# Streams ordered by a per-form time estimate, gather steps paced in that time

## The chip, the cores and the metric

The kernel runs on one core of a Trainium2 chip. The metric is device microseconds of one execution. Its engines are PE (TensorE, matmuls), DVE (VectorE), ACT (ScalarE), POOL (GpSimd, which issues the gathers) and SP (which issues most loads). Each engine works through its own list of instructions in order; semaphores hold an instruction until what it reads is there.

## The reference, cut to what matters

One layer over 1024 tokens of width 1024, in float32:

```
x += W_out [ gated delta rule, 4 heads of 128, chunks | RG-LRU, 512 channels ](norm(x))
x += cross attention, 4 heads, into 256 memory tokens (norm(x))
x += PEER(norm(x)):
    sc = q . subkeys            # 8 heads x 2 halves x 128 keys
    top 16 of each half, top 16 of their sums -> 16 experts a head, 128 a token
    out = sum_e gate_e * gelu(u[e] . h) * v[e]      # u, v: 16384 x 1024
out = norm(x)
```

## The kernel before

The kernel is written as Python generators, called streams, which emit instructions piece by piece. A function `together` picks which stream emits next, while the program is built. A tile scheduler behind it may still move single instructions; what it makes of them is each engine's list.

**The front.** The stream `mixed` runs four mixers of 256 tokens (mixer 0 to 3). A mixer projects (`pj`), convolves, and then solves two chunks of 128 tokens one after the other. A chunk is a chain: a triangular inverse in levels of `gd` matmuls (operands `TT`, `Xi`, `Y`, `W`), whose results go through ACT copies (`Xi`, `Y`) and one DVE product (`W`, a 128x512 row) before the next matmuls can start. At its end stand `g`, `St`, `go` on DVE and a transposition (`tp<-identf,go`), and then the output projection, whose results DVE adds to `X`. Side streams do the RG-LRU channels. The stream `attended` does the cross attention and then the product-key queries (`pj<-hT,w` on PE, `sc`, top-16 searches `s`, `i`, `mr` on DVE) for units of tokens at 0, 128, 256, 512 and 768, each as soon as the mixer is through with it. After a unit a stream `choose` runs `select` on DVE (`cand`, `best`, `pos`, `mr`, `oh`, `e`), 128 tokens at a time: the final top 16 and the expert indices.

**Two ways to the experts.** Tokens 256 to 767 go the dense way. The stream `gated` builds with one-hot rows (`oh<-iot,e1T`, `oh<-keys,e2T` on DVE, `ohg` on ACT, `gd<-ohg,oh` on PE) a table of gates, which goes through `stage` to DRAM; this part is called the gates. Then `dense` runs 128 pieces, each with 24 `dh` and on average 24 `po` matmuls of 512 columns, in which every expert is computed for all 512 tokens. The other four blocks of 128 tokens (0, 128, 768, 896) go by gather steps, 256 a block, 1024 in all: POOL gathers 128 rows of u or v (512 KB) into one of six row buffers `rb`, and DVE does one row on it (SCALAR_TENSOR_TENSOR `rb`, 128x1024).

**What sets the order.** While it emits, the program keeps a clock of its own for each engine: `pe.at`, `act.at`, `dve.at`. `spend` adds an instruction's time, a fixed part and a rate by elements, from when its inputs are known; a result counts as known `HOP` later. `together` gives the turn to a stream whose time has come, by rank and by how much PE time it has had. `Paced.tick` adds up PE's time and emits a gather step (`step`) whenever another `pace` of it has passed: in the front of the time on the clock, waits too (`real`), in the dense phase of the matmuls' own time. `PACES` has one pace for each mixer, `PACE_G` that of the gates, `PACE_D` that of the dense phase. Steps left at the end run by themselves.

Of the kernel before, what the change touches and what calls it, by code (L numbers as in the profile page):

```python
# [8 lines left out]
F = mybir.dt.float32  # L9
BF = mybir.dt.bfloat16  # L10
# [3 lines left out]
AF = mybir.ActivationFunctionType  # L14
# [4 lines left out]
S = 1024  # L19
# [4 lines left out]
TD = 2 * T  # L24
# [9 lines left out]
BIG = 3.0e38  # L34
NROW = 6
RANK = (1, 1, 1, 0)
HOP, SLACK, WAIT = 100.0, 8000.0, 1000.0
SHARE = (6.0, 1.0, 6.0, 1.0)
L_NORM, L_STEP, L_CONV, L_SOFT, L_GATE = 14000.0, 2500.0, 4000.0, 6000.0, 1500.0
PACES = (2800.0, 2800.0, 2800.0, 3500.0)  # L40
PACE_G, PACE_D = 3500.0, 2250.0
FIRST = 0
EARLY = T
UNITS = ((0, 1), (128, 1), (256, 2), (512, 2), (768, 2))
CB = 2
# [4 lines left out]
def block_kernel(ctx: ExitStack, tc: tile.TileContext, a):  # L50
    nc = tc.nc
# [8 lines left out]
    def known(x):  # L60
        lo, hi = part(x)
        return max([t for (l, h), t in written.get(x.tensor.name, {}).items() if l <= hi and h >= lo],
                   default=0.0)

    def wrote(x, t):
        written.setdefault(x.tensor.name, {})[part(x)] = t

    def moved(n):
        dma[0] = max(dma[0], pe.at) + n / 360.0
        return dma[0] + 2000.0  # L70

    class Engine:

        def __init__(self, engine, fixed, rate):
            self.engine, self.fixed, self.rate = engine, fixed, rate
            self.at = self.total = self.end = 0.0

        def __getattr__(self, op):
            call = getattr(self.engine, op)

            def f(*args, **kw):
                r = call(*args, **kw)  # L82
                aps = [x for x in list(args) + list(kw.values()) if isinstance(x, bass.AP)]
                if op == "dma_start":
                    moved(prod(args[0].shape) * 4)
                else:
                    self.spend(aps)
                return r
            return f

        def spend(self, aps, n=0):
            t0 = max([self.at] + [known(x) for x in aps[1:]])
            ns = self.fixed + self.rate * (n or max(prod(x.shape[1:]) for x in aps))
            self.at = t0 + ns
            self.end = max(self.end, self.at)
            self.total += ns
            wrote(aps[0], self.at + HOP)

    class Paced(Engine):

        def __init__(self):
            super().__init__(nc.tensor, 0.0, 0.0)
            self.ns, self.pace, self.real = 0.0, PACES[0], True

        def matmul(self, out, l, r, **kw):
            self.engine.matmul(out, l, r, **kw)  # L106
            self.rate = 1.67 if r.dtype == F else 0.42
            self.tick([out, l, r])

        def transpose(self, out, i, ident):  # L110
            self.engine.transpose(out, i, ident)  # L111
            self.rate = 0.43
            self.tick([out, i])

        def tick(self, aps):
            t = self.at, self.total
            self.spend(aps, prod(aps[-1].shape[1:]))
            self.ns += self.at - t[0] if self.real else self.total - t[1]
            while self.ns > self.pace and (not self.real or dve.at < self.at + SLACK and not late_row()):
                self.ns -= self.pace  # L120
                step()

    pe = Paced()
    sp = Engine(nc.sync, 0.0, 0.0)
    act, dve = Engine(nc.scalar, 200.0, 0.72), Engine(nc.vector, 68.0, 1.04)

    consts = ctx.enter_context(tc.tile_pool(name="consts", bufs=1))
    small = ctx.enter_context(tc.tile_pool(name="small", bufs=2))
# [54 lines left out]
    def to_all(src, n):  # L183
        return bass.AP(tensor=src.tensor, offset=src.offset, ap=[[0, 128], [1, n]])
# [98 lines left out]
    def low(i):  # L283

        return early[:, 2 * i:2 * i + 2, :].rearrange("p s (c t) -> p (s c) t", c=D // T)
# [28 lines left out]
    def mm3(out, l, r, start, stop):  # L314
        pe.matmul(out, l[0], r[0], start=start, stop=False)
        pe.matmul(out, l[0], r[1], start=False, stop=False)
        pe.matmul(out, l[1], r[0], start=False, stop=stop)
# [96 lines left out]
    def mixer(fp, t0, qkv):  # L414
# [13 lines left out]
        hT = fp.tile([128, 8, T], F, name="hT", bufs=1)  # L428
        if t0 < EARLY:
            hT = Pair(hT, low(0), tmp)  # L430
# [4 lines left out]
        for c in range(8):  # L435
            if t0 < EARLY:
                mm3(ps[:8, :T], (wabh[:, c, :], wabl[:, c, :]), (hT.hi[:, c, :], hT.lo[:, c, :]), c == 0, c == 7)
# [85 lines left out]
        def out(b0, b1):  # L523

            while not ready >= {"y", *range(b0, b1)} or t0 and t0 not in read:
                yield None
            if not x1:
                x1.append(att.tile([128, NB, D], F, name="X1", bufs=1))
                sp.dma_start(x1[0], rows(a["x"], t0, NB))
            X = x1[0][:, b0:b1, :]  # L530
            for j in range(8):
                ps = yield from proj("wout", j, y, b1 - b0, b0)
                add_cols(X, j, ps)
            done[t0 + b0 * 128] = X
# [55 lines left out]
        for b in range(NB):  # L590
# [141 lines left out]
            if t0 == 0 and b == 0:  # L732
                yield Stream(out(0, 1), FIRST, SHARE[0])

# [368 lines left out]

    todo, fetched = [], []
    blocks = {}

    def add_block(row, rs, idx, gt):
# [5 lines left out]
    def row_of(i):  # L1115
        if not place:
            rb = gat.tile([128, NROW + 2, D], F, name="rb")
            place.extend(rb[:, k, :] for k in range(NROW + 2))
        return place[i]

    def slot():
        turn[0] += 1
        return row_of(turn[0] % NROW)

    def fetch():
        row, ph, k = todo.pop(0)
        B = blocks[row]
        if (ph, k) == ("u", 0):
            B["h"] = row_of(NROW)
            sp.dma_start(B["h"], x2d[row:row + 128, :])  # L1130
            B["w"] = slot()
            sp.dma_start(B["w"], to_all(a["wffn"], D))
        t = slot()
        pool.indirect_dma_start(  # L1134
            out=t, out_offset=None, in_=a[ph],
            in_offset=bass.IndirectOffsetOnAxis(ap=B["idx"][:, k:k + 1], axis=0))
        fetched.append((row, ph, k, t, moved(4.0 * 128 * D)))
# [4 lines left out]
    def step():  # L1142
        while todo and len(fetched) < NROW - 1:
            fetch()
        if not fetched:
            return False
        row, ph, k, t, _ = fetched.pop(0)
        B = blocks[row]
        if ph == "u":
            if k == 0:  # L1150
                dve.scalar_tensor_tensor(B["h"], B["h"], B["rs"], B["w"], op0=OP.mult, op1=OP.mult)
                B["hd"] = gat.tile([128, 128], F, name="hdot", bufs=1)
            tc.keep_in_program_order(
                dve.scalar_tensor_tensor(t, t, 1.0, B["h"], op0=OP.mult, op1=OP.mult,
                                         accum_out=B["hd"][:, k:k + 1]))
            if k == 120:
                B["x"] = row_of(NROW + 1)
                sp.dma_start(B["x"], x2d[row:row + 128, :])
            if k == 127:
                B["a"] = gat.tile([128, 128], F, name="ga", bufs=1)  # L1160
                act.activation(B["a"], B["hd"], AF.Gelu_apprx_tanh)
                dve.tensor_mul(B["a"], B["a"], B["gt"].rearrange("p h k -> p (h k)"))
        else:
            tc.keep_in_program_order(
                dve.scalar_tensor_tensor(B["x"], t, B["a"][:, k:k + 1], B["x"], op0=OP.mult, op1=OP.add))
            if k == 127:
                finish(B["x"], row, t)
        return True

    def finish(X, row, jk):  # L1170
        ss = small.tile([128, 1], F, name="f_ss")
        act.activation(jk, X, AF.Square, accum_out=ss)
        dve.tensor_scalar(ss, ss, 1.0 / D, EPS, op0=OP.mult, op1=OP.add)
        r = rsqrt(ss, 1, "f_")
        dve.scalar_tensor_tensor(X, X, r, wfin, op0=OP.mult, op1=OP.mult)
        sp.dma_start(a["out"][row:row + 128, :], X)
# [51 lines left out]
    def mixed():  # L1228

        for i in range(NP):  # L1230
            pe.pace = PACES[i]
            yield from mixer(fp, i * T, qkv)
# [10 lines left out]
    def attended():  # L1243
        yield from memory(att, KT, VM)
        first.rank = FIRST
        for t0, nb in UNITS:
# [17 lines left out]
    fps.close()  # L1264
    with tc.tile_pool(name="dn", bufs=1, side="right") as d2, \
            tc.tile_pool(name="dps", bufs=1, space=bass.MemoryType.PSUM) as dps:
        pe.pace, pe.real = PACE_D, False
        dense(dn[0], d2, dps, hT, raws)
    while step():
        pass  # L1270
# [64 lines left out]
```

## Time and profile before

| | |
|---|---|
| Median of 3 runs | 3278.47 us (3274.97 to 3279.72) |
| The profiled execution | 3275.43 us, its span 3273.7 us |
| PE, DVE, ACT, POOL busy | 91%, 84%, 39%, 44% of the span |
| First `dh` matmul | 1790 us |
| Last `po` matmul ends | 3261 us |

The profile is of one execution, and shares of it are means over stages that differ. The front is everything before the first `dh` matmul. A busy PE is not PE at its peak, since matmuls overlap in the records. Two rows of one engine may overlap by some 0.1 us, so a time from start to start says more than a duration.

### The profile page before, as it was taken

How to read it: one execution, taken by the hardware profiler on the slowest of the kernel's cores; microseconds unless marked ns; L12 is line 12 of the kernel's file. 1: busy time of each engine (PE TensorE's matmuls, PEld its weight loads, DVE VectorE, ACT ScalarE, POOL GpSimd, SP SyncE). 2: the span in 40 equal slices, each digit the busy share in tenths (PEclk: the TensorE clock that was granted, in tenths of full speed). 3: DMA queues.
4: the chain of work that ended last, by engine and by line, in shares of the span. 5: the costliest groups of instructions: out<-in, count | busy, mean ns of one | idle time of the engine just before them, and what ended most of it. 6: DMA issues, size and time to landing. Idle time of an engine off the chain costs nothing.

```text
span 3273.7 us, 46519 instructions
## 1 busy us (share of the span) xinstructions
PE 2987.4 (91%) x16212; PEld 2559.6 (78%) x16212; DVE 2737.6 (84%) x5999; ACT 1277.8 (39%) x2694; POOL 1431.4 (44%) x1046
## 2 busy tenths in 40 slices
PE   6999997699999989898857899999999999999998
PEld 6888887678988878887746677888888878888886
DVE  7634776877787898898999798888999989899998
ACT  6843363236322642376357332222222222222222
POOL 0000233334433344243345375556666655566663
PEclk9999998899999999998968899999999999999999
DMA  5346788688888769888888799999999899999995
GB/s 170 110 143 208 248 281 308 232 285 284 308 292 291 251 223 332 301 281 302 303 289 273 267 329 334 333 340 330 344 333 328 319 334 333 330 341 327 339 331 198
DMA packets 321547, 941.66 MB, mean 288 GB/s; under 512 B 28912, under 2 KB 108832, under 8 KB 319264
## 3 DMA queue, kind: packets, MB, share of 16 engines
q0 software_dynamic: 148048, 538.04, 46.8%
q1 hardware_dynamic: 107216, 367.08, 30.9%
q10 hardware_dynamic: 66048, 33.56, 3.7%
q8 instruction: 128, 2.10, 0.3%
q14 instruction: 107, 0.88, 0.1%
HBM read 894.53 MB, written 44.04 MB: 287 GB/s over the span
## 4 chain that ended last, share of the span: by engine, by line
PE 61%; DVE 20%; DMA 9%; ACT 5%; issue 3%; POOL 1%; SPq 0%; ACTq 0%; DVEq 0%; POOLq 0%
PE dh L106 21%; PE po L106 20%; PE pj L106 15%; DVE rb L82 6%; DMA rb<-in_u,idx 4%; PE gd L106 3%; DVE oh L82 3%; DMA gd<-stage 2%; DMA w<-in_pwq 1%; PE tp L111 1%; PE sc L106 1%; DVE cy L82 1%; ACT ohg L82 1%; DVE i L82 1%; ACT L82 1%
## 5 line engine op out<-in xcount | busy, mean ns | idle before, releaser
L1134 POOL DMA_INDIRECT rb<-in_u,idx x512 | 677.4, 1323 | 1111.9 <-DVE rb L82 497.0
L1134 POOL DMA_INDIRECT rb<-in_v,idx x512 | 745.0, 1455 | 690.3 <-DVE rb L82 478.7
L82 DVE SCALAR_TENSOR_TENSOR rb<-rb 128x1024 f32<-128x1024 f32 x512 | 613.1, 1218 | 90.2 <-DMA rb<-in_u,idx 90.2
L82 DVE SCALAR_TENSOR_TENSOR rb<-rb,ga 128x1024 f32<-128x1024 f32 x512 | 655.0, 1279 | 11.2 <-DMA rb<-in_v,idx 4.9
L106 PE MATMUL pj<-hT,w 128*128 128x256 f32 (+1 forms) x2880 | 590.6, 358 | 16.2 <-DMA w<-in_pwq 11.8
L106 PEld LDWEIGHTS pj<-hT,w 128*128 128x128 f32 x2880 | 491.8, 195 | 73.5 <-DMA w<-in_pwq 13.1
L106 PE MATMUL dh<-hT_h,uh 128*128 128x512 f32 x1024 | 407.1, 398 | 21.4 <-ACT dg L82 20.7
L106 PE MATMUL po<-vh,dah 128*128 128x512 f32 x1024 | 404.8, 395 | 9.7 <-DVE acc L82 8.7
L106 PE MATMUL dh<-hT_l,uh 128*128 128x512 f32 x1024 | 406.2, 397 | 0.0
L106 PE MATMUL dh<-hT_h,ul 128*128 128x512 f32 x1024 | 406.1, 397 | 0.0
L106 PE MATMUL po<-vh,dal 128*128 128x512 f32 x1024 | 405.2, 396 | 0.4 <-DVE dal L82 0.4
L106 PE MATMUL po<-vl,dah 128*128 128x512 f32 x1024 | 405.3, 396 | 0.0
L82 ACT CAST uh<-ur 128x1024 fp32r<-128x1024 f32 x128 | 134.7, 1052 | 561.0 <-PE dh L106 352.8
L106 PE MATMUL gd<-ohg,oh 128*128 128x128 f32 x1024 | 183.7, 332 | 81.4 <-ACT ohg L82 54.5
L106 PEld LDWEIGHTS dh<-hT_h,uh 128*128 128x128 f32 x1024 | 193.2, 189 | 69.3 <-ACT dg L82 21.6
L106 PEld LDWEIGHTS gd<-ohg,oh 128*128 128x128 f32 x1024 | 163.8, 228 | 101.9 <-ACT ohg L82 80.5
L106 PEld LDWEIGHTS po<-vh,dah 128*128 128x128 f32 x1024 | 192.3, 188 | 58.4 <-DVE acc L82 10.0
L106 PEld LDWEIGHTS dh<-hT_h,ul 128*128 128x128 f32 x1024 | 193.0, 189 | 47.0
L106 PEld LDWEIGHTS dh<-hT_l,uh 128*128 128x128 f32 x1024 | 193.2, 189 | 46.4
L106 PEld LDWEIGHTS po<-vl,dah 128*128 128x128 f32 x1024 | 192.3, 188 | 47.2
L106 PEld LDWEIGHTS po<-vh,dal 128*128 128x128 f32 x1024 | 192.3, 188 | 47.1 <-DVE dal L82 0.8
L82 DVE TENSOR_TENSOR ul<-ur,uh 128x1024 fp32r<-128x1024 f32 x128 | 156.0, 1222 | 48.7 <-ACT uh L82 27.6
(339 smaller groups left out, 4757.4 us busy)
## 6 DMA issues: line engine op xcount, KB each, us to landing
ur<-in_ut SPq DMA_DIRECT2D x128, 512.0 KB
vr<-in_v SPq DMA_DIRECT2D x128, 512.0 KB
w<-in_wA SPq DMA_DIRECT2D x80, 512.0 KB
w<-in_pwq SPq DMA_DIRECT2D x80, 512.0 KB
gd<-stage ACTq DMA_DIRECT2D x32, 1024.0 KB
G<-gd SPq DMA_DIRECT2D x16, 2048.0 KB
w<-in_wout SPq DMA_DIRECT2D x40, 512.0 KB
w<-in_wq SPq DMA_DIRECT2D x40, 512.0 KB
```

Source lines behind the costliest of these rows:

```text
L82: r = call(*args, **kw)
L106: self.engine.matmul(out, l, r, **kw)
L111: self.engine.transpose(out, i, ident)
L1134: pool.indirect_dma_start(out=t, out_offset=None, in_=a[ph], in_offset=bass.IndirectOffsetOnAxis(ap=B["idx"][:, k:k + 1], axis=0))
```

## The change

The estimate gets a time for each form of instruction: other fixed parts and rates for DVE, ACT and PE, additions for some operations (`form`), a 1280 ns load when ACT changes its table, a longer `HOP`. It is an estimate at build time alone: no instruction is added for it. The paces are set anew in that time, and the dense phase's pace is worked out, so that the steps that are left are spread over all of it.

```diff
-HOP, SLACK, WAIT = 100.0, 8000.0, 1000.0
+HOP, SLACK, WAIT = 130.0, 8000.0, 1000.0
-PACES = (2800.0, 2800.0, 2800.0, 3500.0)
-PACE_G, PACE_D = 3500.0, 2250.0
+PACES = (3200.0, 3200.0, 3200.0, 4000.0)
+PACE_G, DENSE = 4000.0, 1441000.0
+TABLES = {AF.Exp: (0,), AF.Tanh: (0, 1), AF.Gelu_apprx_tanh: (1,), AF.Sqrt: (2,)}
...
-                    self.spend(aps)
+                    self.spend(aps, *self.form(op, args, kw, aps))
...
+        def form(self, op, args, kw, aps):
+
+            n = max(prod(x.shape[1:]) for x in aps)
+            more = 0.0
+            if self is act:
+                if isinstance(kw.get("scale"), bass.AP):
+                    more += 130.0
+                if "accum_out" in kw:
+                    more += 200.0
+                tables = TABLES.get(args[2]) if len(args) > 2 else None
+                if tables and self.table not in tables:
+                    self.table = tables[0]
+                    more += 1280.0
+            else:
+                if op == "scalar_tensor_tensor":
+                    more += 60.0
+                if "accum_out" in kw or op in ("max_index", "match_replace"):
+                    more += 80.0
+                if op == "tensor_tensor_scan":
+                    n *= 2
+                elif n > 64 and all(x.dtype == BF for x in aps):
+                    n //= 2
+            return n, more
...
-            self.rate = 1.67 if r.dtype == F else 0.42
+            self.rate = 1.7 if r.dtype == F else 0.46
...
-            self.rate = 0.43
+            self.rate = 0.85
...
-    act, dve = Engine(nc.scalar, 200.0, 0.72), Engine(nc.vector, 68.0, 1.04)
+    act, dve = Engine(nc.scalar, 165.0, 0.83), Engine(nc.vector, 150.0, 1.04)
...
+        stepped[0] += 1
...
-        pe.pace, pe.real = PACE_D, False
+        pe.pace, pe.real = DENSE / (2.0 * (S - TD) - stepped[0]), False
```

What it moves is seen in the engines' lists. PE at the end of mixer 3, in the last levels of its second chunk; `pj<-hT,w` and `sc<-subk,pqT` are the product-key queries of unit 512. Before:

```order
L106 MATMUL gd<-Xi,TT 128x128 x3
L106 MATMUL sc<-subk,pqT 128x128 x2
L106 MATMUL pj<-hT,w 128x256 x8
L106 MATMUL gd<-Y,W 128x128 x4
L106 MATMUL sc<-subk,pqT 128x128 x2
L106 MATMUL pj<-hT,w 128x256 x8
L106 MATMUL gd<-St_138,knT 128x128 x4
L106 MATMUL sc<-subk,pqT 128x128 x2
L106 MATMUL pj<-hT,w 128x256 x8
L106 MATMUL gd<-g_11313,Y 128x128 x4
```

The same place of the changed kernel's PE list:

```order
L132 MATMUL gd<-W,Y 128x128 x4
L132 MATMUL gd<-Y,W 128x128 x4
L132 MATMUL gd<-Xi,TT 128x128 x4
L132 MATMUL gd<-W,Y 128x128 x4
L132 MATMUL gd<-Y,W 128x128 x4
L132 MATMUL gd<-Xi,TT 128x128 x4
L132 MATMUL gd<-Y,W 128x128 x4
L132 MATMUL gd<-St_138,knT 128x128 x4
L132 MATMUL gd<-g_11787,Y 128x128 x4
L132 MATMUL gd<-Xi,kd 128x128 x4
```

The queries of unit 512 no longer stand between the links of the chain; they are through before it. On DVE, the changed kernel's list in the same levels has this (`rb,hdot<-rb` are gather steps, `best` and `pos` belong to unit 512's `select`, `W` to the chain), and lumps of six, six and five steps again behind it, ahead of the next `W`, `g` and `St`:

```order
L84 SCALAR_TENSOR_TENSOR rb,hdot<-rb 128x1024 x6
L84 MAX_INDEX pos<-best,cand 128x8
L84 MATCH_REPLACE mr_11688<-best,cand 128x80
L84 TENSOR_TENSOR W<-gd,wm_85 128x512
L84 MAX best<-mr_11688 128x8
L84 MAX best<-cand 128x8
L84 MAX_INDEX pos<-best,mr_11688 128x8
```

The rows of `select` are new there; before, that `select` stood in the gates. At the end of mixer 2, where DVE adds the output projection to `X`, before (`mr`, `s`, `i` belong to the queries of unit 256):

```order
L82 SCALAR_TENSOR_TENSOR rb<-rb,ga 128x1024
L82 MAX_INDEX i_1_8112<-s_1_8110,mr_9906 128x8
L82 SCALAR_TENSOR_TENSOR rb<-rb,ga 128x1024
L82 TENSOR_TENSOR X_8734<-X_8734,pj 128x2x128
L82 SCALAR_TENSOR_TENSOR rb<-rb,ga 128x1024
L82 MAX_INDEX i_0_8111<-s_0_8109,sc 128x8
L82 SCALAR_TENSOR_TENSOR rb<-rb,ga 128x1024
L82 MATCH_REPLACE mr_9939<-s_0_8109,sc 128x128
```

And in the changed kernel (`ii`, `oh` belong to unit 256's `select`):

```order
L84 SCALAR_TENSOR_TENSOR rb<-rb,ga 128x1024
L84 SCALAR_TENSOR_TENSOR ii<-t_10209,low 128x128
L84 SCALAR_TENSOR_TENSOR rb<-rb,ga 128x1024
L84 TENSOR_TENSOR oh<-oh,iota_79 128x1024
L84 SCALAR_TENSOR_TENSOR rb<-rb,ga 128x1024
L84 TENSOR_TENSOR X_8844<-X_8844,pj 128x2x128
L84 SCALAR_TENSOR_TENSOR rb<-rb,ga 128x1024
L84 TENSOR_TENSOR oh<-oh,ib 128x1024
```

Here the queries of unit 256 are through, and its `select` stands in their place.

## Rows read from the trace of the kernel before

**Rows 1.** The page's head: span, and busy time of each engine.
```profile
span 3273.7 us, 46519 instructions
PE 2987.4 (91%) x16212; PEld 2559.6 (78%) x16212; DVE 2737.6 (84%) x5999; ACT 1277.8 (39%) x2694; POOL 1431.4 (44%) x1046
```

**Rows 2.** Windows: stretch, its length, each engine's busy time, clock, DMA share, GB/s.
```profile
core 0: us, PE busy (x) PEld busy (x) DVE busy (x) ACT busy (x) POOL busy (x), PEclk, DMA share, GB/s
0.00:1353.00 1353.00, 1204.48 (x8127) 1098.83 (x8128) 997.51 (x3114) 574.59 (x1387) 380.78 (x342) 0.96 0.72 249
1353.00:1790.00 437.00, 343.04 (x1944) 305.17 (x1944) 404.88 (x1251) 279.79 (x770) 168.04 (x129) 0.86 0.88 290
578.00:675.00 97.00, 67.24 (x474) 63.96 (x473) 78.50 (x281) 19.16 (x39) 36.02 (x32) 0.81 0.71 245
990.00:1127.00 137.00, 132.14 (x831) 116.97 (x830) 107.75 (x261) 63.00 (x163) 45.01 (x39) 1.00 0.77 266
1127.00:1311.00 184.00, 163.93 (x1036) 148.10 (x1035) 166.07 (x595) 72.22 (x160) 74.97 (x60) 0.97 0.79 278
1311.00:1404.00 93.00, 83.43 (x562) 77.34 (x561) 80.10 (x296) 42.12 (x117) 29.51 (x28) 0.93 0.84 284
1404.00:1637.00 233.00, 201.74 (x1216) 180.41 (x1215) 209.47 (x675) 133.21 (x367) 85.99 (x72) 0.93 0.88 302
1637.00:1790.00 153.00, 98.60 (x495) 86.29 (x494) 146.58 (x399) 109.47 (x307) 66.71 (x45) 0.75 0.88 276
1790.00:3261.00 1471.00, 1439.85 (x6144) 1155.64 (x6144) 1326.33 (x1593) 421.15 (x534) 882.57 (x577) 0.99 0.89 323
```

**Rows 3.** The chain that ended last, dense phase: start us, us, what (two pieces apart).
```profile
2042.57 7.00 PE po L106 x30
2064.97 7.00 PE po L106 x30
```

**Rows 4.** PE's waits from 1812 us on, and the chain at the handover.
```profile
PE dh L106 <- ACT dg L82: 20.7, 2, 17.9
PE po L106 <- DVE acc L82: 8.7, 3, 5.2
...
1789.85 21.73 DMA gd<-stage
```

**Rows 5.** Timeline of PE, 1250 to 1268 us: chain without filler.
```profile
1260.57 2.04 PE L106 MATMUL gd<-W,Y 128*128 128x128 f32 x8 [3.31 <-DVE W L82]
1262.41 1.61 PE L106 MATMUL gd<-Y,W 128*128 128x128 f32 x8
1263.86 1.06 PE L106 MATMUL gd<-Xi,TT 128*128 128x128 f32 x8
```

**Rows 6.** Timeline of PE, 1285 to 1297 us: chain with filler.
```profile
1290.69 1.05 PE L106 MATMUL gd<-Y,W 128*128 128x128 f32 x8
...
1292.03 3.62 PE L106 MATMUL pj<-hT,w 128*128 128x256 f32 x16
1295.48 1.05 PE L106 MATMUL gd<-St,knT 128*128 128x128 f32 x8
```

**Rows 7.** Timeline of DVE: gather steps behind each other.
```profile
1254.34 1.22 DVE L82 SCALAR_TENSOR_TENSOR rb<-rb 128x1024 f32<-128x1024 f32 x1
...
1255.48 1.22 DVE L82 SCALAR_TENSOR_TENSOR rb<-rb 128x1024 f32<-128x1024 f32 x1
...
1787.15 5.23 DVE L82 SCALAR_TENSOR_TENSOR rb<-rb,ga 128x1024 f32<-128x1024 f32 x4
```

**Rows 8.** Groups of DVE from 1795 us on: steps on u rows, idle time before them.
```profile
L82 DVE SCALAR_TENSOR_TENSOR rb<-rb 128x1024 f32<-128x1024 f32 x256 | 306.2, 1220 | 49.1 <-DMA rb<-in_u,idx 49.1
```

**Rows 9.** Tiles `best` and `oh` on DVE: duration ns min/median/max, first and last start.
```profile
L82 DVE MAX8 best<-cand x64: 217/229/245, 331.9 to 1734.7; 128x8 f32<-128x80 f32 x64
L82 DVE FIND_INDEX8 pos<-best,cand x64: 225/231/236, 332.2 to 1735.1; 128x8 uint32<-128x80 f32 x64
L82 DVE TENSOR_TENSOR oh<-oh,ib x32: 668/691/706, 344.8 to 1917.1; 128x1024 bf16<-128x1024 bf16 x32
```

More of the change, by code (lines that the diff above doesn't have):

```diff
@@ L76, in __init__ @@
             self.at = self.total = self.end = 0.0
+            self.table = None
         def __getattr__(self, op):
@@ L86, in f, with spend @@
                 else:
-                    self.spend(aps)
+                    self.spend(aps, *self.form(op, args, kw, aps))
                 return r
             return f
-        def spend(self, aps, n=0):
+        def form(self, op, args, kw, aps):
[20 more added lines that the diff above has]
+            return n, more
+        def spend(self, aps, n=0, more=0.0):
             t0 = max([self.at] + [known(x) for x in aps[1:]])
-            ns = self.fixed + self.rate * (n or max(prod(x.shape[1:]) for x in aps))
+            ns = self.fixed + more + self.rate * (n or max(prod(x.shape[1:]) for x in aps))
             self.at = t0 + ns
@@ L1101, in dense @@
         finish(acc, row3, xs[0][:, NT - 1, :])
-    todo, fetched = [], []
+    todo, fetched, stepped = [], [], [0]
     blocks = {}
```

## The prediction

> **What bounds the kernel now.** I read the page first: span 3273.7 us, PE busy 91% of it, DVE 84%, ACT 39% [rows 1]. That average covers stages with different limits, so I next cut the span at the end of the front (the first `dh` matmul, at 1790 us) and the front at the places that the change touches [rows 2]. Read each line of it as a contest between PE's column and DVE's.
>
> The dense phase (1790 to 3261) is PE's: one piece of 48 matmuls repeats every 11.2 us (two pieces in 22.40 us [rows 3]), and 128 pieces take 1433.6 of the 1471 us. DVE is busy for 1326 us there and seldom ends a wait: the 37 us that PE loses are one stop of 17.9 us at the handover, where the last `stage` store lands 21.73 us after its issue, and a few short ones [rows 2 to 4].
>
> The front (0 to 1790) has two regimes. From the first gates row on DVE (1353 to 1790) DVE is busy for 405 of 437 us and PE for 343: DVE's [rows 2]. Before that PE has 1204 of 1353 us and DVE 998; what costs time there is the mixer's chain. Each level of the chunk solve goes matmul, copy by ACT or product by DVE, matmul. Where PE has other work the chain is free: from 1285 us on four `gd` matmuls alternate with eight `pj` matmuls of the attention stream (3.62 us), and PE hardly waits [rows 6]. Where it has none, PE waits for the one DVE row `W` (3.31 us at 1260.57) [rows 5], and whatever stands ahead of `W` in DVE's list is paid by PE. The worst case of now is 578 to 675: the tail of mixer 1 without any filler, 97 us for some 50 us of PE work, DVE busy 78 us [rows 2].
>
> **What the change does, and its price.** No instruction of the computation is added or removed; it changes the order and where the 1024 gather steps (one DVE row each, with its 512 KB gather) stand. Three parts.
>
> *The dense phase gets fewer steps.* Steps are now spread over all of it: 1024 less what is done. In the orders 447 steps stand ahead of the first `dh` matmul before, 484 after: 37 move from the dense phase to the front. Rows of a step start 1.14 us apart for u, and 1.2 us for v (5.23 us for four) [rows 7], so DVE has some 43 us less in the dense phase. That phase is PE's, so it gains at most the 37 us, of which 17.9 hang on a store and stay. The rest sits at the starts of new gather rows (49.1 us of DVE waits for u rows [rows 8]), which stay too, only shorter. I take 5 us off; bounds 0 and 19.
>
> *The front gets them, and not where DVE is free.* I counted steps and `select` rows between the places of PE's list that the stretch ends of [rows 2] mark. `select` of 128 tokens has 8 top-16 searches of five rows of 0.23 to 0.30 us, 24 one-hot rows of up to 0.69 us and some 30 small ones [rows 9]: about 25 us of DVE, 50 for a unit of 256.
>
> Tail of mixer 1 (578 to 675): 51 steps instead of 31, so 20 x 1.15 = 23 us more for DVE in the one place where PE has no filler. DVE's idle 18 us there are chain waits (PE's and ACT's part of each link), which stay. If a fifth of the steps fall into them: +18 us.
>
> End of mixer 2 (990 to 1127): 55 steps instead of 40 (+18 us), and the whole `select` of unit 256 (+49 us), which before stood in 1127 to 1311. DVE goes from 108 to about 174 us against 137 of now: DVE becomes the bound, +37 us. The second order fence of the change section shows it: two or three steps and select rows between two adds of the output projection.
>
> 900 to 1050 us of PE work (1127 to 1311) loses that `select`: DVE falls from 166 to some 120, and the stretch falls from 184 to what PE's 150 us of work take elsewhere in the front, 165: -19 us.
>
> End of mixer 3 (1311 to 1404): here lies the largest term. Before, unit 512's attention ran beside the last chunk, and its `pj` rows are the filler of [rows 6]. After, those rows stand earlier, and the chain stands bare: ten groups of four `gd` in a row, while DVE has lumps of six, six, six and five steps and the first half of unit 512's `select` ahead of the rows that the chain waits for. 53 steps instead of 26 (27 x 1.15 = 31 us), select 46 instead of 4, attention 9 less: DVE 80 becomes some 145. PE can't run ahead of it, so the stretch costs 145 to 150 instead of 93: +55.
>
> Gates (1404 to 1790): the same select no longer stands here (-41 us of DVE), 8 steps fewer (-10), attention 11 more at first and 12 less later. The first part, 233 us, would fall by 35 on DVE alone (41 + 5 - 11), but PE has 175 us of work and ACT 133 in it; I take -30. The second, 153 us, -10: there each group waits on ACT's four `ohg` rows as much as on DVE.
>
> In stretches not named the counts fall by 5 and 8 steps and PE is the bound: 0. Table loads go from 62 to 59 on an ACT that is 39% busy: 0.
>
> Sum: +18 +37 -19 +55 -30 -10 -5 = **+46 us**. The profiled execution took 3275.4 us, so 3321; the median of the three timed runs is 3.0 us higher, so I say 3324.
>
> One thing is left out of the +55. After its wait of 3.31 us PE's next eight `gd` rows took 2.04 us and the eight behind them 1.61, against 1.06 at full rate [rows 5]; the granted clock of 1637 to 1790, with PE busy 64%, is 0.75 [rows 2]. By these rows four lumps cost some 1.5 us each at the lower of the two clock levels (1.2 GHz, half of 2.4), 6 us in all, which may hide beside DVE. The Trainium skill (TensorE: Matmul & The Clock Gate, "What's actually happening") says that the low clock is the default and that only activity releases it. By that the whole bare chain would run at the low level, ten groups at about 1 us more each: +10 instead of +6, and a sum of +56 instead of +52. The trace agrees as far as it goes, since the rate came back within two groups.
>
> **Rivals.**
> *The front absorbs it (faster).* DVE is idle for 355 of the first 1353 us [rows 2]. If the tile scheduler's list order is looser than I read it, and DVE runs the lumps while PE still works through earlier rows, the rows that the three tails gain vanish in that idle time. Then it pays only for the 19 us of PE work that move ahead of the gates, and the gates, DVE's own stage, give back what leaves them: select 41, steps 10, attention 12, some 63 us. 3275 + 20 - 63 - 5 is 3227. It decides as soon as less than 64 of the 110 us of the three tails (18 + 37 + 55) are paid, since the other terms are -64. For it speaks that DVE's total is well under the span; against it, the stretch 578 to 675, where the lumps of now are paid in full. The Trainium skill (Perfetto Trace Analysis, "Optimization Strategy") says that a kernel whose most contended engine changes over time may gain from interleaving the regimes. Moving steps from the dense phase to the front, and select from the gates to the mixer, is that, so by this rule the time would fall as in this rival; [rows 2] show the spare time that it needs, but in chains.
> *Nothing measurable.* The tails cost 58 to 70 us of the 110, and the other terms give that back. 3272 to 3285.
> *Gathers late (much slower).* After a lump of six steps all six row buffers are empty at once, and the next lump needs 3 MB. The dense phase moves 323 GB/s [rows 2], so 9.7 us for it, while the lumps stand some 9 to 12 us apart. If every one of about eight lumps in the three tails waits 5 us for its rows, the sum is +86: 3364.
>
> **Chances and numbers.** My forecast (+46; its own range 3295 to 3350) 0.60, absorbed 0.22, nothing 0.08, gathers late 0.10. About 0.2% (6.6 us) is what a measurement of this kernel can tell from no change. Faster 0.22, same 0.08, slower 0.70. Range: 3245 (which leaves out half of the absorbed case) to 3375 (the late gathers and a little more).
>
> **What would show it.** Right: the first `dh` matmul at 1825 to 1855 instead of 1790; the span between it and the last `po` within 10 us of 1466; near 1400 to 1480 a stretch of 40 us or more in which PE is busy under 50% and waits for DVE (`W`, `g`, `go`), with the clock well below 1; gates shorter than 437 us by 40 or more. Wrong: PE busy above 85% through the end of mixer 3, or a first `dh` before 1785. Late gathers would show as DVE idle before `rb` rows released by DMA inside the tails, 5 us and more at a time.

## The result, and the profile after

| | before | changed |
|---|---|---|
| Median | 3276.72 us (4 runs, 3273.17 to 3279.72) | 3373.71 us (4 runs, 3373.15 to 3373.92) |
| Profiled span | 3273.7 us | 3371.4 us |
| First `dh` matmul | 1790 us | 1899 us |
| Last `po` matmul ends | 3261 us | 3356 us |

The changed kernel is slower: ratio 1.0296, 95% interval 1.0278 to 1.0314, that is +97 us where the prediction has +46. The dense phase, from the first `dh` to the last `po`, is 14 us shorter (1456 instead of 1471), so the loss, 110 us, lies in the front. The page's head, to be held against [rows 1]:

```profile
span 3371.4 us, 46536 instructions
PE 3010.3 (89%) x16212; PEld 2578.1 (76%) x16212; DVE 2744.0 (81%) x5999; ACT 1277.5 (38%) x2691; POOL 1419.2 (42%) x1046
```

DVE has the same 5999 instructions and 6 us more of busy time: no work was added. PE has the same 16212 and 23 us more. Next the windows of the changed kernel, cut where PE has done the same amount of matmul work as at the cuts of [rows 2], and in the same columns:

```profile
579.00:701.00 122.00, 70.55 (x475) 67.13 (x474) 100.57 (x303) 19.54 (x39) 66.61 (x51) 0.73 0.73 252
1013.00:1181.00 168.00, 142.64 (x844) 122.66 (x843) 158.74 (x528) 76.61 (x175) 60.35 (x52) 0.92 0.72 261
1181.00:1370.00 189.00, 162.49 (x978) 145.74 (x977) 130.82 (x406) 60.16 (x154) 69.87 (x62) 0.94 0.81 280
1370.00:1523.00 153.00, 99.53 (x596) 90.98 (x595) 136.18 (x484) 40.98 (x94) 69.55 (x55) 0.78 0.73 254
1523.00:1755.00 232.00, 199.56 (x1245) 181.51 (x1243) 191.53 (x512) 141.80 (x394) 81.98 (x66) 0.93 0.87 287
1755.00:1899.00 144.00, 97.75 (x490) 86.85 (x488) 134.45 (x331) 109.14 (x309) 65.19 (x41) 0.76 0.90 283
1899.00:3356.00 1457.00, 1438.49 (x6144) 1154.37 (x6144) 1278.25 (x1547) 416.84 (x531) 802.54 (x538) 1.00 0.87 312
```

Against [rows 2]: mixer 1's tail 97 to 122, mixer 2's end 137 to 168, the stretch behind it 184 to 189, mixer 3's end 93 to 153, the gates' first part 233 to 232, the second 153 to 144. In mixer 3's end the two kernels do the same amount of matmul work; PE is busy for 99.53 us on it instead of 83.43, at a granted clock of 0.78 instead of 0.93, and DVE is busy for 136 us instead of 80.

What PE waits for there stands in its timeline, 1402 to 1425 us, beside which [rows 5, 6] are the chains of before:

```profile
1403.11 2.05 PE L132 MATMUL gd<-W,Y 128*128 128x128 f32 x8 [6.91 <-DVE best L84]
1404.95 1.91 PE L132 MATMUL gd<-Y,W 128*128 128x128 f32 x8
1406.65 1.21 PE L132 MATMUL gd<-Xi,TT 128*128 128x128 f32 x8
1414.08 2.05 PE L132 MATMUL gd<-Y,W 128*128 128x128 f32 x8 [6.22 <-DVE best L84]
...
1423.05 2.04 PE L132 MATMUL gd<-g,Y 128*128 128x128 f32 x8 [5.46 <-DVE best L84]
```

The releaser named, `best`, is a row of unit 512's `select` that ended last before PE went on; the operand PE wants is `W` or `g`, which stand in DVE's list right beside it. DVE's timeline shows how, 1413 to 1423 us:

```profile
1413.25 0.68 DVE L84 TENSOR_TENSOR W<-gd,wm 128x512 f32<-128x512 f32 x1
1413.85 0.23 DVE L84 MAX8 best<-mr 128x8 f32<-128x80 f32 x1
...
1414.77 0.23 DVE L84 MAX8 best<-cand 128x8 f32<-128x80 f32 x1
1414.92 0.23 DVE L84 MAX8 best<-mr 128x8 f32<-128x80 f32 x1
...
1416.62 1.22 DVE L84 SCALAR_TENSOR_TENSOR rb<-rb 128x1024 f32<-128x1024 f32 x1
...
1417.76 1.22 DVE L84 SCALAR_TENSOR_TENSOR rb<-rb 128x1024 f32<-128x1024 f32 x1
...
1422.56 0.34 DVE L84 SCALAR_TENSOR_TENSOR g<-gd,cgb,vb 128x128 f32<-128x128 f32 x1
```

Between `W` and `g` stand ten rows of `select` and six steps, 9.3 us from start to start. PE has 3.5 us of work in that time (1414.08 to 1417.59) and waits for the rest of it.

The dense phase answers to [rows 3, 4, 8]. The chain that ended last repeats every 22.40 us as before:

```profile
2099.96 7.00 PE po L132 x30
...
2122.36 7.00 PE po L132 x30
```

PE's waits from 1900 us on:

```profile
PE dh L132 <- ACT dg L84: 12.2, 2, 10.8
PE po L132 <- DVE acc L84: 5.2, 3, 2.9
```

The stop at the handover has shrunk from 17.9 to 10.8 us; the other waits stay small.

### The profile page after: what moved, and what is told of

Same layout as the page of the kernel before. It is cut to its first block, busy times and chain, and to the rows that moved or that the text cites. A ratio compares the mean times of both kernels' runs of the same rounds, so it can differ in the third digit from the quotient of the medians.

```text
span 3371.4 us, 46536 instructions
## 1 busy us (share of the span) xinstructions
PE 3010.3 (89%) x16212; PEld 2578.1 (76%) x16212; DVE 2744.0 (81%) x5999; ACT 1277.5 (38%) x2691; POOL 1419.2 (42%) x1046
## 4 chain that ended last, share of the span: by engine, by line
PE 60%; DVE 18%; DMA 10%; issue 7%; ACT 4%; POOL 2%; SPq 0%; DVEq 0%; POOLq 0%; ACTq 0%
PE dh L132 20%; PE po L132 19%; PE pj L132 15%; DVE rb L84 6%; DMA rb<-in_u,idx 5%; PE gd L132 4%; DVE oh L84 2%; POOL rb L1160 2%; DMA rb<-in_v,idx 2%; PE sc L132 2%; DMA w<-in_pwq 1%; PE tp L137 1%; ACT ohg L84 1%; DVE i L84 1%; DVE pos L84 1%
## 5 line engine op out<-in xcount | busy, mean ns | idle before, releaser
L1160 POOL DMA_INDIRECT rb<-in_u,idx x512 | 687.4, 1343 | 1125.9 <-DVE rb L84 515.2
L1160 POOL DMA_INDIRECT rb<-in_v,idx x512 | 722.8, 1412 | 786.8 <-DVE rb L84 578.4
```

The costliest lines, as they stand in the source:

```text
L1160: pool.indirect_dma_start(out=t, out_offset=None, in_=a[ph], in_offset=bass.IndirectOffsetOnAxis(ap=B["idx"][:, k:k + 1], axis=0))
```

## The experiments

Theory 1 is mine: steps and `select` ahead of the chain's rows on DVE are what the tails pay. Its rivals: the number of steps ahead of the dense phase counts, wherever they stand (2), or the dense phase's new pace (3). Theories 4 to 6 came with the first four results: one number of the estimate does it all (4), through the length of a chain's link (5) or through DVE's queue (6). A stretch is always cut at the same PE work as in [rows 2]; steps and searches were counted in each kernel's lists.

| label | median us | ratio to before, 95% interval |
|---|---|---|
| dense_spread_alone | 3279.24 | 0.9985 to 1.0022 |
| new_dve_fixed_alone | 3379.46 | 1.0281 to 1.0329 |
| old_dve_fixed | 3270.78 | 0.9961 to 0.9992 |
| old_fixed_times | 3257.65 | 0.9916 to 0.9950 |
| result_later_only | 3354.21 | 1.0210 to 1.0244 |
| changed_without_steps | 3117.56 | one run |
| before_without_steps | 3073.45 | one run |
| no_steps_mixer3_tail | 3364.64 | 1.0249 to 1.0287 |
| unit512_held_back | 3372.43 | 1.0268 to 1.0302 |
| paced_by_own_time | 3388.86 | 1.0320 to 1.0354 |
| fewer_steps_in_gates | 3271.47 | 0.9955 to 0.9990 |
| no_steps_mixer1_tail | 3303.94 | 1.0041 to 1.0090 |

### Which part of the change does it

**dense_spread_alone**, the kernel before with the spread of what is left:

```diff
-        pe.pace, pe.real = PACE_D, False
+        pe.pace, pe.real = DENSE / (2.0 * (S - TD) - stepped[0]), False
```

> The kernel before with one part of the change alone: the steps that are left are spread over the whole dense phase (same list as before up to the first dh matmul). Theory 1 (the tails of the mixers pay, the dense phase does not): 0, so 3270 to 3283 us, since PE bounds the dense phase either way. Theory 3 (the new dense pace costs a good part of the 97 us, for example because steps now stand in the last pieces): 3295 or more. Were it faster, by 5 us or more, part of the dense phase's gain of 10 us is the spread's.

1.0003 of the time before: the spread does nothing that can be measured, as theory 1 has it. Its front has the same lists as before and so shows what two executions of one list differ by: 190 us instead of 184 in 1127 to 1311, 236 instead of 233 in the gates' first part, and the three tails within 1 us.

**old_fixed_times** and **old_dve_fixed**, the changed kernel with numbers of the estimate taken back, the first both engines', the second DVE's alone:

```diff
-    act, dve = Engine(nc.scalar, 165.0, 0.83), Engine(nc.vector, 150.0, 1.04)
+    act, dve = Engine(nc.scalar, 200.0, 0.72), Engine(nc.vector, 68.0, 1.04)
```

```diff
-    act, dve = Engine(nc.scalar, 165.0, 0.83), Engine(nc.vector, 150.0, 1.04)
+    act, dve = Engine(nc.scalar, 165.0, 0.83), Engine(nc.vector, 68.0, 1.04)
```

> The changed kernel with the old fixed parts and rates of ACT and DVE (200/0.72 and 68/1.04), all else as changed. 32 steps stand in the tail of mixer 1 (51 in the changed kernel), 39 at the end of mixer 2 (55), 25 at the end of mixer 3 (53), with 9 of the 32 searches of unit 512's select there (32); unit 256's select stays at the end of mixer 2. Theory 1 (DVE rows ahead of the chain's rows): the +25 of mixer 1's tail goes, of the +31 of mixer 2's end half stays, of the +60 of mixer 3's end 40 to 50 go: 3285 to 3310 us. Theory 2 (what counts is how many steps stand ahead of the dense phase: 17 fewer than before): 3245 to 3270.

> The changed kernel with one number of the estimate back at its old value: DVE's fixed part, 68 instead of 150. Steps in the tail of mixer 1, at the end of mixer 2 and of mixer 3: 32, 41 and 29 (51, 55 and 53 in the changed kernel; 32, 39 and 25 with all old fixed parts and rates); both selects stand as early as in the changed kernel. Theory 4 (this number alone makes the planner see longer waits in the chains and fill them with steps, and the steps are the cost): 3255 to 3280 us, mixer 3's end at 105 to 125. If the selects' early place is the cost, mixer 3's end stays above 140 and the time above 3300. If the number acts only together with ACT's, 3340 or more.

The loss is gone, and the first beats both kernels, by 0.67% to before. Theory 1 was too high by 27 us for it (3285 at the least); theory 2's range took the time in, but it falls with no_steps_mixer3_tail below, which has 12 steps fewer ahead of the dense phase than before and is 2.7% slower. For the second 3270.78 is inside theory 4's range, with runs from 3258.65 to 3283.19; its profile is of a span of 3256.9 us. Its windows of mixer 1's tail, mixer 2's end, mixer 3's end and the two parts of the gates:

```profile
566.00:662.00 96.00, 66.58 (x479) 63.69 (x478) 79.48 (x282) 19.27 (x39) 35.47 (x31) 0.82 0.70 244
965.00:1115.00 150.00, 136.87 (x841) 119.22 (x840) 141.30 (x505) 70.73 (x170) 47.22 (x40) 0.97 0.74 251
1293.00:1411.00 118.00, 89.25 (x560) 80.58 (x560) 102.80 (x437) 37.90 (x96) 32.86 (x31) 0.86 0.72 236
1411.00:1639.00 228.00, 197.87 (x1242) 180.61 (x1241) 198.53 (x611) 140.39 (x388) 81.26 (x66) 0.91 0.90 293
1639.00:1763.00 124.00, 89.42 (x470) 79.37 (x468) 112.81 (x287) 100.05 (x289) 50.89 (x32) 0.82 0.88 271
```

Both selects stand as early as in the changed kernel; only the steps in the tails are back at 32, 41 and 29. So the early selects alone don't make the loss.

**new_dve_fixed_alone**, the same number in the kernel before:

```diff
-    act, dve = Engine(nc.scalar, 200.0, 0.72), Engine(nc.vector, 68.0, 1.04)
+    act, dve = Engine(nc.scalar, 200.0, 0.72), Engine(nc.vector, 150.0, 1.04)
```

> The kernel before with one number of the change alone: DVE's fixed part in the estimate, 150 instead of 68. Steps in the three places 52, 57 and 35 (31, 40 and 26 before); both selects move to the ends of mixers 2 and 3 as in the changed kernel; 73 more steps ahead of the dense phase. Theory 4: the tail of mixer 1 as in the changed kernel (about 122 us instead of 97), the end of mixer 2 about 168 instead of 137, the end of mixer 3 115 to 140 instead of 93: 3340 to 3380 us. If the number needs the rest of the change, 3265 to 3300.

+3.05%, as much as the whole change, with the tails at 126, 165 and 130 us. Of all the numbers that the change touches, this one makes the loss.

**result_later_only** asks how it does so: DVE's queue by the old number, its results 82 ns later.

```diff
-            wrote(aps[0], self.at + HOP)
+            wrote(aps[0], self.at + HOP + (82.0 if self is dve else 0.0))
...
-    act, dve = Engine(nc.scalar, 165.0, 0.83), Engine(nc.vector, 150.0, 1.04)
+    act, dve = Engine(nc.scalar, 165.0, 0.83), Engine(nc.vector, 68.0, 1.04)
```

> The changed kernel with DVE's fixed part 68 again, but each DVE result counted as known 82 ns later: in the estimate a chain's link is as long as in the changed kernel, while DVE's queue moves on as fast as before. 46, 55 and 47 steps in the three tails (51, 55 and 53 in the changed kernel), both selects early. Theory 5 (the longer links are what draws the steps and the selects into the chains): the tails at 115 to 122, 160 to 168 and 140 to 150 us, 3335 to 3365 us in all. Theory 6 (the number hurts since it counts a row's overlap with the next as queue time): at the time of the kernel with 68, 3255 to 3285.

3354: theory 5. The tails are 119, 164 and 153 us. Most of the loss, 76 us, comes with the length of a chain's link in the estimate. In the front a step is due by time on the clock, waits too, so longer links draw more steps into the chain, where the tails get 46, 55 and 47.

### Order or steps

**changed_without_steps** and **before_without_steps** leave out the gathers and their DVE rows, in the u and the v part alike:

```diff
-            tc.keep_in_program_order(
-                dve.scalar_tensor_tensor(t, t, 1.0, B["h"], op0=OP.mult, op1=OP.mult,
-                                         accum_out=B["hd"][:, k:k + 1]))
+            dve.spend([t]+[t, B["h"], B["hd"][:, k:k + 1]])
```

> The changed kernel without the steps' gathers and DVE rows (the gathered experts' part of four blocks is left out of the result); the planner still spends their time, so that the streams stand nearly as in the changed kernel. The dense phase stays at 1440 to 1465 us. Theory 1 with the steps as the whole cost of the tails: the front (to the first dh matmul) comes within 25 us of that of the kernel before without steps. If the order of the streams (bare chain, selects beside the chains) costs by itself, it stands 50 us or more above.

> The kernel before, without the steps' gathers and DVE rows in the same way (the gathered experts' part is left out). The gates' first part is 200 to 215 us with DVE some 80 us freer if DVE bounds it as my sum had it, and stays at 225 to 233 if PE and the waits for ACT bound it. Mixer 1's tail falls from 97 to 60 to 75 us.

The changed order is 44 us slower even without a step (one execution of each). If that holds with the steps in, 53 of the 97 us are theirs; that the two parts simply add isn't shown, and old_dve_fixed has both selects as early and is as fast as before. These runs also lack the gathers' transfers, so they don't part a step's DVE row from its gather. The two expectations for it (within 25 us, or above 50) both miss. Before, mixer 1's tail is in its range (72), the gates' first part below (195). The windows of mixer 1's tail, mixer 2's end, mixer 3's end and the gates' first part, changed:

```profile
550.00:627.00 77.00, 60.30 (x473) 57.08 (x472) 42.84 (x203) 21.57 (x42) 0.00 (x0) 0.91 0.23 76
919.00:1066.00 147.00, 134.97 (x825) 118.12 (x825) 100.79 (x458) 73.51 (x171) 0.00 (x0) 0.97 0.34 113
1231.00:1342.00 111.00, 87.38 (x581) 80.03 (x580) 83.10 (x397) 42.75 (x98) 1.40 (x2) 0.89 0.31 102
1342.00:1547.00 205.00, 191.55 (x1243) 176.90 (x1242) 129.79 (x517) 135.22 (x387) 0.00 (x0) 0.95 0.59 180
```

and before:

```profile
545.00:617.00 72.00, 58.17 (x474) 56.40 (x474) 43.59 (x219) 20.55 (x41) 0.00 (x0) 0.91 0.30 97
908.00:1041.00 133.00, 131.66 (x837) 117.35 (x836) 63.40 (x213) 62.25 (x160) 0.00 (x0) 1.00 0.36 120
1213.00:1302.00 89.00, 83.62 (x566) 77.36 (x565) 61.65 (x314) 41.79 (x114) 1.40 (x2) 0.94 0.51 161
1302.00:1497.00 195.00, 187.95 (x1213) 172.87 (x1213) 140.61 (x539) 133.13 (x370) 0.00 (x0) 0.97 0.57 175
```

The order costs +5, +14 and +22 in the three places. The last row is the one that my sum lacked: with 69 us less of DVE than in [rows 2] the gates' first part still takes 195 us, since PE alone has 188. And the changed order takes 10 more there, not less: unit 512's `select` is gone from it, but half of unit 768's runs there in its place, and DVE has only 11 us less.

### Taking one tail's cost away

**no_steps_mixer3_tail**: the changed kernel with a flag.

```diff
+            if self.hold:
+                return
             self.ns += self.at - t[0] if self.real else self.total - t[1]
...
+            pe.hold = b == NB - 1 and t0 == 3 * T
```

> The changed kernel, but no step is emitted from the start of mixer 3's second chunk to the end of that mixer (9 stand at its end instead of 53, 43 instead of 60 in the stretch before it; 49 more go to the dense phase, spread). Order of the streams as changed: the chain stays bare. Theory 1: the stretch of mixer 3's end, 153 us in the changed kernel, loses 44 x 1.15 = 51 us of DVE and falls to 100 to 115; the one before it, 189, to 175 to 185; the dense phase stays within 10 us: 3310 to 3335 us. If the bare chain itself was the cost and not the steps in it, the stretch stays above 130 and the time above 3345. If late gathers were it, PE's waits in the stretch go with the steps, too, but DVE's idle before rb rows must have been 20 us or more there in the changed kernel.

The windows of mixer 3's end and of the gates' first part:

```profile
1362.00:1467.00 105.00, 83.66 (x566) 76.75 (x565) 85.77 (x415) 41.34 (x102) 11.02 (x11) 0.90 0.46 155
1467.00:1727.00 260.00, 206.91 (x1242) 189.58 (x1241) 206.60 (x596) 138.12 (x383) 92.93 (x78) 0.85 0.83 279
```

Mixer 3's end is right, 105 us instead of 153; the total is not, 3364.64 instead of 3310 to 3335. The gates took 28 of the 48 us back (79 steps instead of 67 in their first part, 260 us instead of 232), and the dense phase, with 49 steps more, 16.

**unit512_held_back** gives the chain its filler back:

```diff
-            while t0 not in done:
+            while t0 not in done or t0 == 2 * T and "tail" not in done:
```

(`tail` is put into `done` where mixer 3's second chunk begins.)

> The changed kernel, but the attention stream may begin unit 512 only with mixer 3's second chunk, so that its projections and attention stand beside that chunk again and its select in the gates. 25 steps at the end of mixer 3 (53 in the changed kernel), 2 of the 32 searches of the select (32), but 74 steps instead of 60 in the stretch before it and 10 more steps in all ahead of the dense phase. Theory 1 (stream order): the end of mixer 3 falls from 153 to 95 to 115 us, the stretch before it, now with a bare first chunk, grows from 189 to 195 to 210, the gates' first part grows by 0 to 15: 3335 to 3360 us. Theory 2 (number of steps ahead of the dense phase): 3375 to 3400.

The windows of the stretch ahead, mixer 3's end and the gates' first part:

```profile
1183.00:1400.00 217.00, 170.18 (x1135) 156.79 (x1134) 131.75 (x314) 65.03 (x157) 92.95 (x77) 0.89 0.77 265
1400.00:1496.00 96.00, 83.75 (x496) 76.20 (x496) 89.98 (x367) 49.77 (x134) 30.90 (x26) 0.92 0.88 295
1496.00:1741.00 245.00, 206.82 (x1207) 185.59 (x1206) 224.49 (x673) 137.16 (x371) 103.67 (x80) 0.90 0.87 299
```

Again the place is right (96 us) and the total is missed: the stretch ahead grew by 28 and the gates by 13. The filler that covers one chain bares another.

**paced_by_own_time** counts PE's own time in the front:

```diff
-            self.ns += self.at - t[0] if self.real else self.total - t[1]
+            self.ns += self.total - t[1]
```

(with paces of 2200, 2200, 2200, 2500 and 2100.)

> The changed kernel, but in the front the pace is counted in PE's own time, not in the time on the clock with its waits (paces 2200, 2200, 2200, 2500 and 2100, so that about as many steps as in the changed kernel stand ahead of the dense phase: 532 rows instead of 537). 31, 56 and 39 in the three tails, both selects early. Theory 5 (steps counted into planned waits are the cost of the tails beside the streams' order): mixer 1's tail back at 95 to 100, mixer 3's end at 125 to 135, the rest as in the changed kernel: 3310 to 3345 us. If the number of steps ahead of the dense phase counts and not where they stand, 3365 to 3380.

Mixer 1's tail is 99 us, mixer 3's end 138, little above the expected 125 to 135; the total is a miss, 3388.86. The steps went to the gates: 82 in their first part, which takes 261 us.

**fewer_steps_in_gates** and **no_steps_mixer1_tail** start from old_fixed_times. The first has `PACE_G` at 6000; the second has the flag above with `t0 == T`, and 4500 for mixer 3 and `PACE_G`.

> The changed kernel with the old fixed parts and rates of ACT and DVE, and a pace of 6000 in the gates: 39 steps fewer in the gates, 42 more in the dense phase. My runs without steps let a step cost some 0.5 us in the gates and 0.2 in the dense phase: 3257.7 - 20 + 8 = 3246, 3238 to 3254. If the gates' length is PE's and ACT's, as it looked after the first runs, it is 3257 to 3270.

> The changed kernel with the old fixed parts and rates of ACT and DVE, no step from the start of mixer 1's second chunk to that mixer's end, and paces of 4500 in mixer 3 and the gates: 0, 49 and 25 steps in the three tails, 13 of 32 searches of unit 512's select at mixer 3's end, 62 steps more in the dense phase. Theory 1: mixer 1's tail at 72 to 78 us (77 without any steps) instead of 98, 10 more in the stretch ahead of it, the dense phase up to 15 longer: 3225 to 3250 us. If the tail's length is the bare chain's and not the steps', 3255 or more.

Both missed, 3271.47 and 3303.94, at the same place. The gates' first part and the dense phase of old_fixed_times and of the first, then mixer 1's tail and the dense phase of the second:

```profile
1399.00:1625.00 226.00, 195.72 (x1229) 178.71 (x1228) 214.89 (x728) 138.45 (x380) 81.68 (x66) 0.92 0.92 303
1763.00:3239.00 1476.00, 1444.23 (x6144) 1157.78 (x6144) 1341.65 (x1599) 421.39 (x533) 902.94 (x594) 0.99 0.90 328
```

```profile
1397.00:1623.00 226.00, 198.45 (x1226) 181.28 (x1225) 185.04 (x654) 136.77 (x377) 44.81 (x40) 0.92 0.75 235
1746.00:3252.00 1506.00, 1458.28 (x6143) 1159.42 (x6144) 1394.32 (x1641) 422.33 (x535) 978.36 (x636) 0.99 0.92 337
```

```profile
561.00:628.00 67.00, 57.28 (x475) 55.87 (x474) 44.41 (x221) 18.14 (x38) 0.00 (x0) 0.90 0.31 108
1738.00:3290.00 1552.00, 1474.31 (x6144) 1167.63 (x6144) 1416.78 (x1689) 422.05 (x536) 998.45 (x656) 0.98 0.91 334
```

The gates' first part has 27 steps fewer in the first and keeps its 226 us, as the second half of its expectation has it; the second part gave 15 us (138 to 123). The tail without steps is 67 us, below the 72 to 78 expected. But with 42 and 62 more gathers than in old_fixed_times the dense phase grew by 30 and 76 us. In the second PE waited there 50.2 us for DVE's `acc`, against 5.2 in the changed kernel.

### What a step costs, over all runs

Steps in a stretch (from the lists) and its length in us. At the mixers' ends only kernels with the same `select` there are taken; the gates' row has both orders, the dense row POOL's gathers from the windows.

| stretch | steps: us |
|---|---|
| mixer 1's tail | 0: 67, 72, 77; 31 or 32: 96 to 99; 46: 119; 51 or 52: 120 to 126 |
| mixer 2's end | 0: 147; 39: 141, 144; 41: 150; 49: 165; 55 to 57: 163 to 169 |
| mixer 3's end | 0: 111; 9: 105; 29: 118; 35: 130; 39: 138; 47: 153; 53: 153 |
| gates, first part | 0: 195, 205; 40: 226; 59 to 71: 226 to 236; 77: 245; 79: 260; 82: 261; 90: 246 |
| dense phase | 538: 1456; 577: 1471, 1471; 594: 1476; 636: 1506; 656: 1552 |

Mixer 2's end and the dense phase take steps at little cost up to a point, some 40 and some 600, and then grow steeply (150 us at 41 steps and 165 at 49; 1476 at 594, 1506 at 636 and 1552 at 656). In the gates' first part the first 40 cost 21 to 31 us, the next 30 at most 10, and beyond some 70 it is longer again; but there the count doesn't decide alone, since 79 steps take 260 us (no_steps_mixer3_tail, mostly steps on u, with 22.0 us of DVE waits for their gathers) and 90 take 246 (new_dve_fixed_alone, mostly on v, 5.2 us). The bare chain of mixer 1's tail charges from the start: 0.8 us a step up to 31 (72 to 97 us) and 1.25 beyond (97 to 122 for 20 more). Mixer 3's end lies between, 105 to 118 us up to 29 steps and 153 from 47 on. The kernel before stands at 40, 71 and 577, just below the three points (at mixer 2's end without a `select` beside the steps). The change went past the first, and past 31 in the bare tail; no_steps_mixer3_tail and paced_by_own_time went past the second, the last two kernels past the third. So what a step costs is shown place by place; but the three runs that kept the new estimate and moved steps or the filler out of one tail (no_steps_mixer3_tail, unit512_held_back, paced_by_own_time) got 9 us of the total back at most, and only the estimate's number brought the loss and took it away.

## Why the prediction was right in sign and small in size

**The three tails: right.** +18, +37 and +55 were predicted, +25, +31 and +60 came, 116 us against 110, with the waits foreseen: PE waits for DVE rows of `W`, `g` and `go` in a bare chain, behind lumps of six steps and `select`. Without steps the order alone pays 41 us in these places; the rest would be the steps', if the two add.

**The dense phase: right.** -14 against -5 (bounds 0 and 19); the stop at the handover gave 7 of it.

**The two returns: the step that failed.** The sum has -19 for 1127 to 1311 and -30 for the gates' first part; measured +5 and -1. That is 53 us, and the gap between +46 and +97 is 51. The -30 rests on two readings: that DVE's column sets the length of the gates' first part, and that "PE has 175 us of work" there. [Rows 2] show PE busy for 201.74 of 233 us; I had taken its matmuls at their best rate, and even with no wait left at all 31 us were the most that could go. DVE gave up 18 us there and not 35 ([rows 2] 209.47, now 191.53), and nothing came of it: PE has the same work (199.56 us) and still waits for 32 us, most of it for rows of DVE and ACT:

```profile
PE gd L132 <- DVE oh L84: 9.4, 4, 6.0
PE gd L132 <- ACT ohg L84: 8.8, 8, 3.3
PE tp L137 <- ACT oT L84: 6.0, 2, 5.6
```

What the runs showed in place of a bound by DVE: 226 to 236 us with anything from 40 to 71 steps, 195 without any. From old_fixed_times to fewer_steps_in_gates DVE loses 30 us of work there (214.89 to 185.04), and the part takes 226 us in both.

In 1127 to 1311 the order alone does give something back: without steps the same PE work takes 172 us before and 164 changed. With them it takes 184 and 189; 5 us are within what one list varies by (dense_spread_alone has 190), but the return is missing, although DVE fell as forecast (166.07 to 130.82 us). More gathers arrive late there. DVE's waits, before:

```profile
DVE rb L82 <- DMA rb<-in_u,idx: 8.1, 5, 3.3
```

and changed:

```profile
DVE rb L84 <- DMA rb<-in_u,idx: 28.2, 16, 4.5
```

One of them stands ahead of rows that PE's longest wait there hangs on (`oT` needs `n_y`, and `n_y` needs `n_ss`):

```profile
1297.62 1.23 DVE L84 SCALAR_TENSOR_TENSOR rb<-rb 128x1024 f32<-128x1024 f32 x1 [4.30 <-DMA rb<-in_u,idx]
1300.52 0.16 DVE L84 TENSOR_SCALAR n_ss<-n_ss 128x2 f32<-128x2 f32 x1
1304.09 0.69 PE L137 MATMUL tp<-identf,oT 128*128 128x128 f32 x2 [9.00 <-ACT oT L84]
```

What `n_ss` reads of ACT was there at 1296.57 (the end of `hT`), so by my estimate some 4 of the 9.00 us are the late gather's. That is the rival of the late gathers, in a place where I didn't look for it; how much of the missing 19 us it makes wasn't tried apart. Inside the three tails, where I did, DVE waited 9.6, 3.0 and 10.1 us for gathers (3.9 at most at a time), against 10.6, 0 and 2.0 before, so there it is a small part.

**What was to show it.** First `dh` at 1825 to 1855: no, 1899. The dense span within 10 us of 1466: yes, 1456, at the edge. A stretch of 40 us near 1400 to 1480 with PE below 50% and a low clock: yes, 1407 to 1447 has PE busy for 14.63 of 40 us, at 0.58. Gates shorter by 40: no; from their first row on DVE (1487) to the first `dh` it is 412 us instead of 437.

**The rivals.** The front didn't absorb it. That rival leaned on the Trainium skill (Perfetto Trace Analysis, "Optimization Strategy"), by which interleaving regimes may gain. It did not here: DVE is busy for 1452.85 of the changed kernel's first 1897 us and so has idle time, but by the table above a stretch takes steps cheaply only up to its own point, and a bare chain not even so.

**A reading that was off.** [Rows 7] have four steps on v in 5.23 us, which is 1.3 us from start to start and not 1.2; no term of the sum moves by it.

**The clock.** Left out of the +55 as 6 us, 10 by the rule of the Trainium skill. PE's busy time for the same work grew by 3.3, 10.5 and 16.1 us in the three tails ([rows 2] against the windows above), 30 in all, of which an unknown part lies beside DVE's rows. The Trainium skill (TensorE: Matmul & The Clock Gate, "What's actually happening") says that the low clock is the default and that activity releases it. The timeline agrees: after every wait of 5 to 7 us the next eight `gd` rows took 2.05 us instead of the 1.06 of [rows 5], half the rate, which is the lower of the two clock levels (1.2 and 2.4 GHz), and only the third group was near it (1.21).

**What stays open.** Why the changed order without steps takes 10 us more in the gates' first part wasn't tried apart. Nor was it shown how a link that is 82 ns longer in the estimate also makes the selects stand earlier; it is seen in the lists alone.

## What to carry to other kernels

An estimate that orders work is a control, not a description: check it by the order that it makes, not by how well it fits the trace. Before booking a return, take the stretch's floor from busy rows of the engine that stays (PE 201.74 of 233 here), not from work at its best rate, and ask which waits stay when the other engine's column falls. And a cheap filler is cheap only up to a count that differs by stretch: list count against length before moving it, or what leaves one place is paid in the next.

## What the runs showed of the hardware

DVE rows overlap by 0.08 us where the next one doesn't read the result. `W` (512 columns) takes 0.68 us in the trace and the row behind it starts after 0.60 (1413.25 to 1413.85); a search's MAX8 takes 0.23 and its neighbour starts after 0.15 (1414.77 to 1414.92); a step takes 1.22 and the next starts after 1.14 (1416.62 to 1417.76). Where the next row does read it, there is no overlap: a step on v adds to the row that the one before it wrote, takes 1.28 us, and four of them stand 1.32 us apart ([rows 7], 5.23 us for four), but the row behind one starts after 1.20 where it doesn't need the result (1782.88 to 1784.08 us, before). Two rows of a short chain show the same, `n_t` and then `n_y`, 0.20 us apart at 0.16 each (1301.32 and 1301.52 us, changed).

The old estimate has 68 + 1.04 x 512 = 600 ns for `W` and 151 for MAX8: start to start. The new one has 682 and 233: the durations. The Trainium skill (Perfetto Trace Analysis, "Optimizing Scalar/DVE Operations") says that profiled latency is about twice the overhead that keeps the engine busy, because the end of one instruction overlaps the next. The trace agrees: the fixed parts that fit the two readings are 68 and 150 ns. Here the longer number hurt mostly through the links: result_later_only, with the queue by starts and the link by durations, is the estimate nearest to these rows, and still loses 76 us.

Nor had I expected how sharp the dense phase's bound is. From 594 gathers (old_fixed_times) to 656 it has the same matmuls and DVE is busy for 91% in both (1341.65 of 1476 us, 1416.78 of 1552), yet it grows by 76 us. The bytes moved (GB/s times length) go from 484 to 518 MB, the rate from 328 to 334 GB/s, and DVE's waits for gathers from 64 to 94 us; its `acc` rows then come late for PE. A bound by the transfers fits that, but so does one by DVE, whose busy time grew by 75 us itself; it wasn't tried apart.
